# Background pieces spread by cost, GpSimd's sums on VectorE and ScalarE, and VectorE's products one matrix product later, in a four-layer encoder

## The chip, the cores and the metric

One core of a Trainium2 chip runs the whole program. Its engines are TensorE (PE in the views, PEld for its weight loads), VectorE (DVE), ScalarE (ACT) and GpSimd (POOL); SyncE (SP) issues the transfers between HBM and the on-chip memory. Each engine runs its own instructions in the order in which the program wrote them, and waits at an instruction until what that needs is there. The metric is the device time of one execution in microseconds (us), the median of several.

## The reference, cut to what matters

Four residual layers work on x of 512 positions by 1024 channels, in float32. Each is a token mixer (Fourier, S5 state space, dilated attention, Fourier) and then a dense SwiGLU layer of inner width 2816.

```python
def swiglu(h, w_gate_up, w_down):
    gate, up = jnp.split(h @ w_gate_up, 2, axis=-1)
    return (jax.nn.silu(gate) * up) @ w_down

for i in range(DEPTH):
    kind = i % N_MIXERS
    h = rms_norm(x, norm_mix_g[i])
    ... # Fourier, S5 or attention
    x = x + mix.astype(x.dtype)
    h = rms_norm(x, norm_ffn_g[i])
    x = x + swiglu(h, ffn_w_gate_up[i], ffn_w_down[i]).astype(x.dtype)
```

The S5 mixer also needs tables that hang on its parameters alone (powers of the complex eigenvalues times the input and output matrices, one set for each of 16 groups of four state blocks).

## The kernel before, in words

The activations stay in on-chip memory with channels on the partitions, X[:, m] being 128 channels by 512 positions, m = 0 to 7. The order on every engine is the order of the code. The plan is Fourier 0, feed-forward 0, S5, feed-forward 1, attention, feed-forward 2, Fourier 1, feed-forward 3.

**Products in two parts.** A float32 value is held as a high part of fewer bits and a low part, and a product is three matmuls (`mm3`, L338 to L340): high by high, high weight by low activation, low weight by high activation. `Stream` brings the weights in chunks of 128x1024: a transfer fills one of three raw buffers `wch`, ScalarE copies the high part into `whi` (L198), VectorE subtracts it to get `wlo` (L199), three buffers each. `next()` gives the chunk that is due and first splits up to two further ones. A transfer into a raw buffer waits until the split of the chunk three before it is done.

**Feed-forward layer (`ffn`).** Two halves. Each half has 11 pairs of products, gate f and up f, with one chunk and 24 matmuls each, into one of four accumulators `pg`. After both, VectorE scales each by the norm (L480, L483), ScalarE takes the SiLU; a product later VectorE multiplies them (L506), ScalarE copies the high part, and GpSimd subtracts to get the low part (L508) of `act`. Then come 8 down products of 33 matmuls, each added to X (L496) at its end; in the second half `after_x` prepares the next layer: squares on ScalarE (L399), their sum `acc` on GpSimd for m = 1 to 6 (L404, on VectorE for the last), and the scaled copy of X for the next layer (HH, high and low part: L434, L425; H for Fourier and S5). `norm_r` takes the sum of `acc` over the channels (L455) after the first two products of the next layer.

**Background.** The S5 tables are made inside feed-forward 0, the attention's bias tables inside feed-forward 1. They are a list of closures; `run_bg`, called after each of the 54 first slots (a slot is one product), runs about one of them. The S5 list is six pieces that ran in Fourier 0 (`run_front`), 14 pieces of set-up, and 40 half-steps: for group b, the loads come at step b, `inputs` (tables `wout`, `mph`) two steps on, `readers` (`bd`, `ce`) in the second half of that step, `lags` (48 small matmuls on TensorE, L974, and the stores) at step b+3, and the last stores at b+4.

**Fourier layer.** Two small transforms, and then for each m a pair of products `pq` and `pp`. ScalarE copies `pq` out (L691), GpSimd makes X - q and X + mirrored q (L693, L694), VectorE adds `pp` (L697, L698). GpSimd also folds the weights (`wplus`, L531).

## Time and profile before

| | |
|---|---|
| median of 3 runs | 2417.97 us (2413.87 to 2418.07) |
| the profiled execution | 2416.0 us |
| its span on the core | 2414.1 us |
| TensorE busy | 2327.1 us, 96% of the span |
| VectorE busy | 1361.5 us, 56% |
| ScalarE busy | 867.5 us, 36% |
| GpSimd busy | 274.9 us, 11% |

The busy shares are averages over stages with different limits, so they say little by themselves: each stage has to be read by its own stretch. The ends of matmuls are modelled, so a busy TensorE need not be one at its peak; what tells is the time that the same number of matmuls takes in two stretches, and the waits.

### The profile page before, as it was taken

What the parts mean: (1) busy time and instruction counts of PE and PEld (TensorE: products, weight loads), DVE (VectorE), ACT (ScalarE), POOL (GpSimd) and SP (SyncE); (2) the same over time, 40 slices, a digit from 0 to 9 for tenths busy, and PEclk for the clock granted to TensorE, in tenths of its full rate; (3) what the DMA queues carried; (4) which work ended last, traced back from release to release, by engine and by line L of the source; (5) the groups of instructions that cost most, each with busy time, mean ns of one, the idle gap of its engine ahead of it and who ended that gap; (6) DMA issues with size and microseconds to landing.
All of it is one profiled execution on the core that took longest, in us unless ns stands there. A gap on an engine that the chain in (4) does not pass through costs nothing.

```text
span 2414.1 us, 32242 instructions
## 1 busy us (share of the span) xinstructions
PE 2327.1 (96%) x12858; PEld 1925.5 (80%) x12858; DVE 1361.5 (56%) x2265; ACT 867.5 (36%) x1531; POOL 274.9 (11%) x213
## 2 busy tenths in 40 slices
PE   9999988968999999999999999999999999999999
PEld 7787766857878888889878987777888887888887
DVE  7878899487543333454576647774433337443332
ACT  3332222534233223244556446544322322322231
POOL 4210000152101001100000000002100115110110
PEclk9999999989999999999999999999999999999999
DMA  4257777783335444322232323232222232222222
GB/s 157 79 152 224 246 240 223 234 281 119 105 96 136 116 123 126 103 90 88 73 95 80 110 78 92 82 88 96 96 96 96 96 113 71 96 96 96 96 96 88
DMA packets 116490, 293.79 MB, mean 122 GB/s; under 512 B 23105, under 2 KB 50020, under 8 KB 116340
## 3 DMA queue, kind: packets, MB, share of 16 engines
q1 hardware_dynamic: 114804, 288.04, 38.3%
q10 hardware_dynamic: 1536, 3.70, 0.5%
q8 instruction: 101, 1.65, 0.3%
q14 instruction: 49, 0.40, 0.1%
HBM read 259.68 MB, written 36.21 MB: 123 GB/s over the span
## 4 chain that ended last, share of the span: by engine, by line
PE 81%; DVE 10%; DMA 3%; issue 2%; ACT 2%; SPq 1%; POOL 1%; ACTq 0%; DVEq 0%; POOLq 0%
PE pg L338 23%; PE pg L339 22%; PE pg L340 22%; PE pg L1392 2%; PE pg L1393 2%; PE pg L1394 2%; DVE wlo L199 1%; DMA s5ZS<-lt 1%; PE pt L1468 1%; PE pt L1510 1%; DVE ms L1113 1%; PE pt L628 1%; DVE ce L739 1%; PE pg L628 1%; PE pg L1435 1%
## 5 line engine op out<-in xcount | busy, mean ns | idle before, releaser
L199 DVE TENSOR_TENSOR wlo<-w,whi 128x1024 fp32r<-128x1024 f32 x360 | 450.8, 1255 | 574.7 <-ACT whi L198 574.7
L340 PE MATMUL pg<-HH,wlo 128*128 128x512 f32 x1792 | 703.2, 392 | 16.2 <-DVE wlo L199 16.2
L338 PE MATMUL pg<-HH,whi 128*128 128x512 f32 x1792 | 709.8, 396 | 3.4 <-DVE HH L434 3.4
L339 PE MATMUL pg<-HH,whi 128*128 128x512 f32 x1792 | 702.4, 392 | 2.0 <-DVE HH L425 2.0
L198 ACT CAST whi<-w 128x1024 fp32r<-128x1024 f32 x360 | 376.9, 1049 | 531.8 <-PE pg L339 420.1
L340 PEld LDWEIGHTS pg<-HH,wlo 128*128 128x128 f32 x1792 | 339.0, 189 | 91.3 <-DVE wlo L199 20.0
L338 PEld LDWEIGHTS pg<-HH,whi 128*128 128x128 f32 x1792 | 338.8, 189 | 81.2 <-DVE HH L434 5.2
L339 PEld LDWEIGHTS pg<-HH,whi 128*128 128x128 f32 x1792 | 339.0, 189 | 74.0 <-DVE HH L425 3.7
L340 PE MATMUL pg<-act,wlo 128*128 128x512 f32 x704 | 274.1, 389 | 1.0 <-DVE wlo L199 0.8
L339 PE MATMUL pg<-act,whi 128*128 128x512 f32 x704 | 274.1, 389 | 0.9 <-POOL act L508 0.9
L338 PE MATMUL pg<-act,whi 128*128 128x512 f32 x704 | 274.5, 390 | 0.0
L508 POOL TENSOR_TENSOR act<-t,act 128x512 fp32r<-128x512 f32 x88 | 115.8, 1316 | 1151.6 <-ACT act L507 1122.7
L483 DVE TENSOR_TENSOR t<-pg,r 128x512 f32<-128x512 f32 x88 | 60.6, 689 | 171.6 <-PE pg L340 171.6
L404 POOL TENSOR_TENSOR acc<-acc,sq 128x512 f32<-128x512 f32 x42 | 61.8, 1470 | 826.4 <-ACT sq L399 826.0
L340 PEld LDWEIGHTS pg<-act,wlo 128*128 128x128 f32 x704 | 132.1, 188 | 29.3 <-DVE wlo L199 1.8
L339 PEld LDWEIGHTS pg<-act,whi 128*128 128x128 f32 x704 | 132.1, 188 | 28.5 <-POOL act L508 1.2
L338 PEld LDWEIGHTS pg<-act,whi 128*128 128x128 f32 x704 | 132.1, 188 | 28.2 <-issue 0.9
L481 ACT ACTIVATE t<-t 128x512 f32<-128x512 f32 x88 | 55.7, 632 | 224.7 <-DVE t L480 224.7
L507 ACT CAST act<-t 128x512 fp32r<-128x512 f32 x88 | 54.7, 621 | 209.1 <-DVE t L506 209.1
L496 DVE TENSOR_TENSOR X<-X,pg 128x512 f32<-128x512 f32 x64 | 43.8, 685 | 89.3 <-PE pg L340 89.3
L1392 PE MATMUL pg<-whi,HH 128*128 128x256 f32 (+1 forms) x256 | 88.2, 344 | 0.0
L1393 PE MATMUL pg<-whi,HH 128*128 128x256 f32 (+1 forms) x256 | 87.1, 340 | 0.0
(331 smaller groups left out, 2723.5 us busy)
## 6 DMA issues: line engine op xcount, KB each, us to landing
w<-in_wgu_dram SPq DMA_DIRECT2D x176, 512.0 KB
w<-in_wdn_dram SPq DMA_DIRECT2D x88, 512.0 KB
w<-in_wqk_dram SPq DMA_DIRECT2D x48, 512.0 KB
w<-in_wv_dram SPq DMA_DIRECT2D x24, 512.0 KB
xpw<-s5SC SPq DMA_DIRECT2D x16, 512.0 KB
xbj<-in_bj_dram SPq DMA_DIRECT2D x16, 512.0 KB
s5WE<-wout SPq DMA_DIRECT2D x16, 512.0 KB
s5YW<-ce SPq DMA_DIRECT2D x16, 512.0 KB
```

The lines of the kernel that those rows point to most:

```text
L198: nc.scalar.copy(hi, t)
L199: nc.vector.tensor_tensor(lo, t, hi, ALU.subtract)
L338: mm(ps, wh, hh, start=first, stop=False)
L339: mm(ps, wh, hl, start=False, stop=False)
L340: mm(ps, wl, hh, start=False, stop=last)
L404: eng.tensor_tensor(self.acc, self.acc, sq, ALU.add)
L481: nc.scalar.activation(t1, t1, AF.Silu)
L483: nc.vector.tensor_tensor(t2, pp[1], self.r, ALU.mult)
L507: nc.scalar.copy(hi, t1)
L508: nc.gpsimd.tensor_tensor(lo, t1, hi, ALU.subtract)
L1392: mm(ps, x, wh[:, k], start=(kk == 0 and t % tb == 0), stop=False, skip_group_check=True)
L1393: mm(ps, y, wh[:, k], start=False, stop=False, skip_group_check=True)
```

## The change

What it does:

- Every background piece has a cost. `run_bg` gives 3 units of room to a gate or up slot, 5 to a down slot, and spreads the list over both halves up to the fourth down product of the second (`BG_ROOM`). An S5 half-step costs 5; the set-up pieces 31 together.
- The scaling of the up product, the multiplication and the low part come one product later than the scaling of the gate product. The low part is on VectorE.
- The low parts of weight chunks (`wlo`) are written after the products and the background piece of a slot (`hold`, `late_low`), no longer right behind the high part.
- A down product is added to X after the matmuls of the next one are written.
- GpSimd's other sums go to VectorE: `acc`, the fold `wplus`, the two sums of the Fourier layer, which now read `pq` directly. In the Fourier layer ScalarE makes the high part of HH, and four squares and sums come after the loop.
- The phases `mph` of the tables are made on ScalarE, four instructions for a group, one step earlier; the signs of `bd`, the copy of the lags and the last stores move to steps of their own.

```diff
+BG_ROOM = (3, 5, 4)
...
-        return len(r) < n or r[-n] < (self.nsplit if tag == "wch" and self.loaders[r[-n]][1] else free)
+        return len(r) < n or r[-n] < (self.nlow if tag == "wch" and self.loaders[r[-n]][1] else free)
...
-                nc.vector.tensor_tensor(lo, t, hi, ALU.subtract)
+                self.lows.append((lo, t, hi))
...
+            if not self.hold:
+                self.low()
+
+    def low(self):
+
+        while self.lows:
+            self.nc.vector.tensor_tensor(*self.lows.pop(0), ALU.subtract)
+        self.nlow = self.nsplit
+
+    def late_low(self):
+        self.low()
+        self._load(self.nuse - 1)
...
+    def run_bg(self, slots, down=False):
+
+        a, b, rest = BG_ROOM
+        self.due += self.total * (b if down else a) / ((4 * FH - 2) * a + (KT + rest) * b) if slots > 1 else self.total
+        while self.bg and self.due > 0:
+            cost, go = self.bg.pop(0)
+            self.due -= cost
+            go()
...
-            eng = nc.vector if m >= (7 if defer else KT - 1) else nc.gpsimd
-            eng.tensor_tensor(self.acc, self.acc, sq, ALU.add)
+            nc.vector.tensor_tensor(self.acc, self.acc, sq, ALU.add)
...
+            def product():
+
                 while late:
-                    self.split_mul(*late.pop())
+                    hi, lo, t1, ps = late.pop()
+                    t2 = wk.tile([P, S], F32, name="t2", tag="t2")
+                    nc.vector.tensor_tensor(t2, ps, self.r, ALU.mult)
+                    nc.vector.tensor_tensor(t1, t1, t2, ALU.mult)
+                    nc.scalar.copy(hi, t1)
+                    lows.append((lo, t1, hi))
+
+            def rest():
+
+                while lows:
+                    nc.vector.tensor_tensor(*lows.pop(), ALU.subtract)
...
             for hf in range(2):
+                self.stream.hold = True
                 for f in range(FH):
                     left = (2 - hf) * (2 * FH + KT) - 2 * f
-                    pp = [self.gemm(self.Hi, self.Lo)]
-                    finish()
+                    pg = self.gemm(self.Hi, self.Lo)
+                    product()
                     if f < FH - 1:
                         self.run_bg(left)
-                    pp.append(self.gemm(self.Hi, self.Lo))
+                    self.stream.late_low()
+                    pu = self.gemm(self.Hi, self.Lo)
...
-                    nc.vector.tensor_tensor(t1, pp[0], self.r, ALU.mult)
+                    nc.vector.tensor_tensor(t1, pg, self.r, ALU.mult)
                     nc.scalar.activation(t1, t1, AF.Silu)
...
+                    rest()
+                    late.append((act[:, 0, f, :], act[:, 1, f, :], t1, pu))
                     self.run_bg(left - 1)
+                    self.stream.late_low()
...
-                    if hf == 1 and m == 3 and nxt and nxt[1] == "s5":
+                    if m:
+                        result(m - 1, done, hf)
+                    self.run_bg((2 - hf) * (2 * FH + KT) - 2 * FH - m, True)
+                    if hf == 1 and m == 4 and nxt and nxt[1] == "s5":
                         self.s5_open()
...
-        nc.gpsimd.tensor_tensor(lo, t1, hi, ALU.subtract)
...
-                nc.gpsimd.tensor_tensor(wp[:, c], ta, tb, ALU.add)
+                nc.vector.tensor_tensor(wp[:, c], ta, tb, ALU.add)
...
-                nc.gpsimd.tensor_tensor(t1[:, 0:257], X[:, m, 0:257], q, ALU.subtract)
-                nc.gpsimd.tensor_tensor(t1[:, 257:512], X[:, m, 257:512], q[:, 255:0:-1], ALU.add)
...
+                nc.vector.tensor_tensor(t1[:, 0:257], X[:, m, 0:257], pq, ALU.subtract)
+                nc.vector.tensor_tensor(t1[:, 257:512], X[:, m, 257:512], pq[:, 255:0:-1], ALU.add)
...
+                squares.append(self.after_x(m, nxt, late=pool2, defer=True))
+                if m < 4:
+                    squares.pop(0)()
...
+                nc.scalar.activation(ph[:, g], sm["iota"], AF.Copy, scale=sm["phi0"][:, 4 * b + g:4 * b + g + 1])
...
-            tt(V, ph, phi.unsqueeze(2).to_broadcast([P, 4, 64]), sm["iota"].unsqueeze(1).to_broadcast([P, 4, 64]), M)
...
+        for i in range(22):
+            cost = 2 if i < 2 else 5 if i < 18 else 0.5
+            out.append((cost, step(i, ((4, lag_rows), (3, signs), (1, phases), (5, store), (2, inputs)))))
+            out.append((cost, step(i, ((3, lags), (4, lag_own), (5, spread), (2, readers), (0, loads)))))
```

How the order moves, first on VectorE in the second half of feed-forward 0, around one `inputs` half-step. In the kernel before, one slot from one weight split to the next:

```order
418 L199 TENSOR_TENSOR wlo<-w_2212,whi 128x1024
419 L506 TENSOR_TENSOR t_2371<-t_2371,t_2374 128x512
420 L739 TENSOR_TENSOR mph<-s5phi_316,c_iota 128x256
421 L931 TENSOR_SCALAR wtmp<-mph 128x4x64
422 L739 TENSOR_TENSOR mph<-mph,wtmp 128x256
423 L739 TENSOR_TENSOR wout<-xpw,xbj 128x4x128
424 L739 TENSOR_TENSOR wtmp<-xpw,xbj 128x512
425 L739 TENSOR_TENSOR wout<-wout,wtmp 128x4x128
426 L739 TENSOR_TENSOR wout<-xpw,xbj 128x4x128
427 L739 TENSOR_TENSOR wtmp<-xpw,xbj 128x512
428 L739 TENSOR_TENSOR wout<-wout,wtmp 128x4x128
429 L199 TENSOR_TENSOR wlo<-w_2297,whi 128x1024
```

In the changed kernel, a slot without a piece and then the slot of an `inputs` half-step:

```order
450 L214 TENSOR_TENSOR wlo<-w_2196,whi 128x1024
451 L520 TENSOR_TENSOR t_2494<-pg,r 128x512
452 L214 TENSOR_TENSOR wlo<-w_2253,whi 128x1024
453 L491 TENSOR_TENSOR t_2528<-pg,r 128x512
454 L492 TENSOR_TENSOR t_2494<-t_2494,t_2528 128x512
455 L967 TENSOR_SCALAR wtmp<-mph 128x4x64
456 L773 TENSOR_TENSOR mph<-mph,wtmp 128x256
457 L773 TENSOR_TENSOR wout<-xpw,xbj 128x4x128
458 L773 TENSOR_TENSOR wtmp<-xpw,xbj 128x512
459 L773 TENSOR_TENSOR wout<-wout,wtmp 128x4x128
460 L773 TENSOR_TENSOR wout<-xpw,xbj 128x4x128
461 L773 TENSOR_TENSOR wtmp<-xpw,xbj 128x512
```

The piece has lost its first instruction, and one slot in three now has no piece; before, every slot here had one. The scaling of the up product (L483, a row of the slot before this one in the old order) stands beside the multiplication.

On VectorE in the Fourier 0 layer, the sums of one m; in the kernel before:

```order
76 L199 TENSOR_TENSOR wlo<-w_391,whi 128x1024
77 L697 TENSOR_TENSOR X<-t_509,pt 128x257
78 L698 TENSOR_TENSOR X<-t_509,pt 128x255
79 L434 TENSOR_SCALAR HH<-X,c_gf 128x512
80 L425 SCALAR_TENSOR_TENSOR HH<-X,c_gf,HH 128x512
81 L789 TENSOR_SCALAR s5k<-s5a 128x128
```

and in the changed kernel:

```order
84 L214 TENSOR_TENSOR wlo<-w_391,whi 128x1024
85 L727 TENSOR_TENSOR t_503<-X,pg 128x257
86 L728 TENSOR_TENSOR t_503<-X,pg 128x255
87 L729 TENSOR_TENSOR X<-t_503,pt 128x257
88 L730 TENSOR_TENSOR X<-t_503,pt 128x255
89 L446 SCALAR_TENSOR_TENSOR HH<-X,c_gf,HH 128x512
90 L425 TENSOR_TENSOR acc<-acc,sq 128x512
91 L823 TENSOR_SCALAR s5k<-s5a 128x128
```

Two sums and an `acc` have come in, and the high part of HH (L434) has left.

On ScalarE in the last down products of feed-forward 0, where the phases `mt` of the S5 layer are turned into sines; in the kernel before (`whi` of chunks 72 and 73 are the layer's last two):

```order
206 L1023 ACTIVATE mt<-mt 128x512
207 L1024 ACTIVATE mt<-mt,c_cols 128x512
208 L198 CAST whi<-w_3933 128x1024
209 L198 CAST whi<-w_3970 128x1024
210 L399 ACTIVATE sq<-X 128x512
211 L1022 ACTIVATE mt<-mt 128x512
```

and in the changed kernel:

```order
210 L421 ACTIVATE sq<-X 128x512
211 L202 CAST whi<-w_3865 128x1024
212 L202 CAST whi<-w_3944 128x1024
213 L421 ACTIVATE sq<-X 128x512
214 L1072 ACTIVATE mt<-mt 128x512
215 L1073 ACTIVATE mt<-mt 128x512
```

Nine of the 24 `mt` instructions stood ahead of the two copies; now all stand behind them.

## Rows read from the trace of the kernel before

**Rows 1.** The page: the chain that ended last, shares of the span by engine.

```profile
PE 81%; DVE 10%; DMA 3%; issue 2%; ACT 2%; SPq 1%; POOL 1%; ACTq 0%; DVEq 0%; POOLq 0%
```

**Rows 2.** Windows: stretch, its length, busy (instructions), TensorE clock, DMA share, GB/s.

```profile
59.70:81.70 22.00, 16.59 (x52) 10.85 (x51) 20.53 (x39) 6.31 (x9) 8.93 (x8) 0.77 0.14 48
81.70:191.10 109.40, 109.40 (x486) 90.16 (x488) 85.59 (x167) 36.45 (x49) 12.82 (x11) 1.00 0.42 129
192.00:257.00 65.00, 64.17 (x416) 51.77 (x412) 58.18 (x102) 18.41 (x35) 2.58 (x2) 1.00 0.79 253
258.00:421.00 163.00, 142.67 (x1014) 110.98 (x1010) 151.65 (x263) 44.56 (x95) 12.99 (x9) 0.96 0.75 237
421.00:431.00 10.00, 8.94 (x81) 6.52 (x79) 6.62 (x8) 4.72 (x6) 2.58 (x2) 1.00 0.37 112
1754.90:1814.90 60.00, 60.00 (x266) 49.69 (x265) 19.66 (x21) 12.36 (x13) 1.29 (x1) 1.00 0.29 97
1814.70:1934.50 119.80, 119.80 (x530) 99.22 (x529) 47.19 (x54) 36.32 (x43) 12.89 (x10) 1.00 0.29 97
1994.50:2050.20 55.70, 53.61 (x265) 43.18 (x264) 41.03 (x69) 17.39 (x38) 33.99 (x26) 0.94 0.23 75
```

**Rows 3.** Waits of TensorE from 258 to 431 us: total, times, longest.

```profile
PE pg L340 <- DVE wlo L199: 16.2, 9, 2.4
```

**Rows 4.** Waits of TensorE from 59.7 to 82 us.

```profile
PE pg L338 <- DVE HH L434: 3.4, 2, 3.0
PE pg L339 <- DVE HH L425: 2.0, 2, 1.1
```

**Rows 5.** VectorE's instructions from 258 to 421 us: busy us, mean ns.

```profile
L199 DVE TENSOR_TENSOR wlo<-w,whi 128x1024 fp32r<-128x1024 f32 x22 | 26.8, 1218 | 0.0
L739 DVE TENSOR_TENSOR wout<-xpw,xbj 128x512 f32<-128x512 f32 x20 | 20.3, 1013 | 0.0
...
L739 DVE TENSOR_TENSOR wtmp<-xpw,xbj 128x512 f32<-128x512 f32 x20 | 13.6, 681 | 0.0
...
L480 DVE TENSOR_TENSOR t<-pg,r 128x512 f32<-128x512 f32 x10 | 6.8, 684 | 0.0
...
L739 DVE TENSOR_TENSOR mph<-s5phi,c_iota 128x256 f32<-128x256 f32 x10 | 4.2, 422 | 5.5 <-DMA s5PH<-mph 5.5
```

**Rows 6.** Timeline at 345 us, GpSimd and VectorE: start, length.

```profile
345.68 1.49 POOL L508 TENSOR_TENSOR act<-t,act 128x512 fp32r<-128x512 f32 x1 [14.16 <-ACT act L507]
...
345.94 1.78 DVE L739 TENSOR_TENSOR wout<-xpw,xbj 128x512 f32<-128x512 f32 x1
```

**Rows 7.** Timeline of TensorE around one block of `lags`.

```profile
280.93 0.39 PE L340 MATMUL pg<-HH,wlo 128*128 128x512 f32 x1
...
282.28 0.50 PE L338 MATMUL pg<-HH,whi 128*128 128x512 f32 x1
```

**Rows 8.** Timeline of VectorE around two set-up pieces (their first row, and what follows).

```profile
75.14 0.22 DVE L797 TENSOR_SCALAR s5mag<-s5rr 128x128 f32<-128x128 f32 x1
...
79.80 1.22 DVE L199 TENSOR_TENSOR wlo<-w,whi 128x1024 fp32r<-128x1024 f32 x1
```

**Rows 9.** Timeline where attention passes to feed-forward 2, GpSimd and TensorE.

```profile
1636.12 8.13 POOL L404 TENSOR_TENSOR acc<-acc,sq 128x512 f32<-128x512 f32 x6 [608.47 <-ACT sq L399]
...
1645.04 0.70 PE L455 MATMUL pt<-acc,c_ones 128*128 128x512 f32 x1 [2.59 <-DVE acc L404]
```

**Rows 10.** Timeline where Fourier 1 begins, VectorE and TensorE.

```profile
1997.29 4.79 DVE L410 TENSOR_SCALAR H<-X,c_gm 128x257 f32<-128x257 f32 x2
...
2002.14 0.80 PE L543 MATMUL pg<-c_cdft,H 128*128 128x128 f32 x2 [1.61 <-DVE H L410]
```

**Rows 11.** Timeline of ScalarE before S5.

```profile
468.48 1.98 ACT L198 CAST whi<-w 128x1024 fp32r<-128x1024 f32 x2
...
482.74 0.72 ACT L1024 ACTIVATE mt<-mt,c_cols 128x512 f32<-128x512 f32 x1
484.56 0.63 ACT L399 ACTIVATE sq<-X 128x512 f32<-128x512 f32 x1 [1.09 <-DVE X L496]
```

More of the change, by code (lines that the diff above doesn't have):

```diff
@@ L213, in next @@
         n = self.nuse
+        if n + count > self.nlow:
+            self.low()
         if ahead:
@@ L317, in set_bg @@
     def set_bg(self, closures):
-        self.bg, self.bg0, self.due, self.slots = list(closures), closures, 0, 4 * FH + KT + 2
-    def run_bg(self, slots):
-        self.due += len(self.bg0) / self.slots if slots > 1 else len(self.bg0)
-        while self.bg and len(self.bg0) - len(self.bg) < self.due:
-            self.bg.pop(0)()
+        self.bg, self.due, self.total = list(closures), 0, sum(c for c, _ in closures)
+    def run_bg(self, slots, down=False):
[5 more added lines that the diff above has]
+            go()
     def run_front(self):
         if self.front:
-            self.front.pop(0)()
+            self.front.pop(0)[1]()
     def keep_warm(self, count):
@@ L920, in c, with phases @@
             return d["bc"][:, 2 + i].unsqueeze(2).to_broadcast([P, 4, 8, 16])
+        def phases(b):
+            ph = tmp[b]["ph"] = tl("mph", [P, 4, 64], 3)
+            for g in range(4):
+                nc.scalar.activation(ph[:, g], sm["iota"], AF.Copy, scale=sm["phi0"][:, 4 * b + g:4 * b + g + 1])
         def inputs(b):
@@ L960, in readers, with signs @@
                 tt(V, ce[:, :, ri], ce[:, :, ri], t, Sb)
+        def signs(b):
+            bd = sm[f"bd{b % 2}"]
+            for di in range(2):
+                hs = slice(64 * di, 64 * di + 64)
+                for ri in range(2):
+                    nc.scalar.activation(bd[hs, 1 + di, ri, :, 0:16], bd[hs, 0, ri, :, 0:16], AF.Copy,
+                                         scale=1.0 - 2.0 * ri)
         def lags(b):
@@ L981, in lags, with lag_rows, lag_own, store @@
             nc.sync.dma_start(self.YW[k, h], ce.rearrange("p g r e q -> p (g r e q)"))
-        def last(b):
+        def lag_rows(b):
+            d = tmp[b]
+            lt = d["lt"] = tl("lt", [P, 256], 2)
+            cut = [t.rearrange("p (a x) -> p a x", a=2)[:, :, 0:112] for t in (lt, d["ps"])]
+            nc.scalar.copy(*cut)
+        def lag_own(b):
+            d = tmp[b]
+            tt(V, d["lt"][:, 112:128], d["ps"][:, 112:128], sm["dd"][:, b], A)
+        def store(b):
             k, h = divmod(b, 2)
@@ L1307, in attn_prepare @@
         out = [load, lambda: None, rows(0), rows(1), rows(2)]
-        return out + [copies(g, i) for g in range(3) for i in range(8)] + [st.close]
+        out += [copies(g, i) for g in range(3) for i in range(8)] + [st.close]
+        return [(1, f) for f in out]
     @staticmethod
```

71 lines of the change are left out of this document (26 added, 45 removed).

## The prediction

> **What bounds the kernel now.** I read the page first. TensorE holds 81% of the chain that ended last, so a gain can only come from stretches where it waits or runs at a lower clock [rows 1]. The windows then show where these are, since the four feed-forward layers do the same products. In feed-forward 2 the second half's 22 gate and up products take 119.8 us and its 8 down products 60.0, at full clock [rows 2]: 5.45 us a product, 7.5 a down product. The same 22 products of feed-forward 0 take 163.0 us. 11 blocks of `lags` lie between them; a block puts 1.35 us between two matmuls that else start 0.23 apart [rows 7], so 1.1 each, 12.1 in all. 163.0 - 119.8 - 12.1 = 31.1 us are lost. The waits say to whom: TensorE waits 16.2 us for the low parts of weights, nine times, all from VectorE [rows 3]. The mean clock of 0.96 (it has two levels, 2.4 and 1.2 GHz, and falls to the lower behind some of these waits) costs about 163.0 x 0.04 = 6.5 more. VectorE is busy 151.65 of the 163.0, so it is the bound there, and nowhere else for as long: in the first half's 109.4 us it was busy 85.59 and TensorE lost nothing [rows 2].
>
> Three smaller losses. The opening of feed-forward 0 takes 22.0 us for two products, 10.9 at full speed: 11.1 lost, 5.4 of it waiting for HH [rows 4], the rest clock (0.77). From 421 to 431 us, 10.0 for a down product (7.5) and a block (1.1): 1.4 lost. From 192 to 257 us, 65.0 for 60.0 and four blocks: 0.6. All told 44 us of feed-forward 0. Outside it, feed-forward 2 begins with a wait of 2.59 us for `acc` [rows 9], and Fourier 1 with one of 1.61 for H [rows 10].
>
> **The even spread (largest term).** The list is 31 units of set-up and 172 of half-steps, 203. The room is 42 x 3 + 12 x 5 = 186, so a gate or up slot gets 203 x 3 / 186 = 3.27 units and a down slot 5.5; before, each slot of the second half got a whole half-step (5 units). Three products then hold one group (10 units), where two held it.
>
> What a group costs VectorE: of the 151.65 us, splits take 26.8, the two scalings and the multiplication, alike in shape, 6.8 each [rows 5]; 104.5 is left for 10.5 groups, 10.0 each. Two parts of that vanish. The first `mph` goes to ScalarE (4.2 / 10 = 0.42; ScalarE is busy 44.56 of 163.0, so four instructions a group hide there). And GpSimd stops holding VectorE up: a `wout` that starts inside GpSimd's 1.49 us instruction takes 1.78 us [rows 6]. The mean is 1013 ns for `wout` and 681 for `wtmp`, which has the same shape [rows 5], so 0.33 x 20 = 6.6 us here, 0.63 a group. That leaves 8.95. Three products then ask of VectorE 8.95 + 3 splits of 1.22 + six sums of 0.684 (per pair two scalings, one multiplication and the low part that comes from GpSimd) = 16.7 us, and of TensorE 3 x 5.45 + 1.1 = 17.4. So VectorE drops just below TensorE, with 4% to spare.
>
> The pieces stay lumps: a slot with one holds 4.5 + 1.4 + 1.2 = 7.1 us, two in a row 14.2 against 12.0 of TensorE, and then one of 2.6. This is covered, since the split made in a product's slot is wanted two products (10.9 us) later. If that cover were gone, each group would cost 2 us. VectorE's waits for TensorE shrink as well: the up product's scaling, which stood ahead of the piece, now comes a product later, when its matmuls are done. I leave 2 us lost of the 31.1 (bounds 0 and 22, the latter under the first rival): **-29**. The 1.4 and 0.6 go too: the low part of `act` is then made in 0.68 instead of 1.49 and is wanted only at the end of the first down product. **-2.0**.
>
> The transfers gain the same evenness. The down products of the first half take five groups instead of four; they ran at 253 GB/s and a share of 0.79, so this rises to about 0.9. It stays below one, and weights are asked for two products ahead.
>
> **The opening of feed-forward 0.** VectorE comes out of the Fourier tail earlier, as it is no longer held up, and the wait for the last HH should shrink to about 1 us. But the set-up now comes three times as dense: 4 units took 75.14 to 79.80, 4.66 us [rows 8], so 3.27 units are 3.8, and with 1.4 of sums and a split of 1.2 a slot asks 6.4 us against 5.45. Over 31 / 3.27 = 9.5 slots this is 9 us behind. The cover is thin at the layer's start, and one or two falls of the clock add to it; the wait for HH and the cover that there is take off as much. So I put the loss at 9 instead of 11.1 (bounds 1, if most is covered, and 14): **-2.1**.
>
> **GpSimd's other sums.** Ahead of feed-forward 2 six sums take 8.13 us on GpSimd [rows 9]; on VectorE, at 0.68 each, they keep up with the squares (0.63, [rows 11]), so `acc` is there before TensorE asks: **-2.6** (1.5 to 3.2). At the start of Fourier 1 two H instructions take 4.79 us [rows 10] while GpSimd folds weights; with the folds behind them the wait of 1.61 goes, and of the clock's loss (55.7 x 0.06 = 3.3 over the stretch) about a quarter: **-2.5** (1.6 to 3.5). In the tail VectorE takes on 16 half-wide sums (6.4 at 0.4), seven of `acc` (4.8) and four folds (4.9), less eight high parts: 41.03 + 16 - 5 = 52 of 55.7 us, and less again as it is not held up. So it stays off the path, where TensorE is. One fold now stands ahead of VectorE's first work on the path in Fourier 0: **+0.5** (0 to 1.2).
>
> **The order on ScalarE before S5.** The nine `mt` instructions that stood ahead of the last two weight copies (468.48) now follow them. The second copy cannot begin before the matmuls of its buffer's last chunk end, three chunks (16.4 us) before the layer's end, so the copies end about where they began before, at 468.5. The 24 `mt` and two squares behind them last some 17.2 us, to 485.7, where the last square began at 484.56 [rows 11]. S5 needs that square: **+1.2** (0 to 3).
>
> **The sum.** -29.1 - 2.0 - 2.1 - 2.6 - 2.5 + 0.5 + 1.2 = -36.6 from the execution's 2416.0 (span 2414.1 and 1.9 around it) is 2379.4. The median of the three runs is 2.0 above that execution, so I say 2380.
>
> **Rivals.** First: VectorE stays the bound through the whole layer. It now idles 7% of the 163.0 us though it is the bound; if it goes on doing so, 16.7 becomes 18.0, and if GpSimd's hold were not the cause of the long `wout`, 18.7. That is 1.3 us over TensorE's 17.4 for each of 17 groups, 22 us lost instead of 2: 2400. The thin 4% speaks for it; that the idling came with waits which the new order takes away speaks against. The Trainium skill (Perfetto Trace Analysis, Optimizing Scalar/DVE Operations) says that a saturated VectorE may be relieved by moving work to ScalarE or GpSimd, though it doubts the latter because the two share a port; the change moves work the other way, and by the first half of that rule it would end near this rival, by the rows on `wout` near the forecast. Chance 18%.
>
> Second: the spread does not do what it is for. If TensorE waits for each lump, not for the average, the 16 groups cost 1.8 us each (16.2 / 9) wherever they stand; 29 us come back, and the time is 2408 to 2416. Against it: in the first half, where some half-steps already ran in slots of the old order, TensorE lost nothing in 109.4 us. 6%.
>
> Third, slower than before: VectorE pays GpSimd's price for what it takes over. The place is the two Fourier layers: 41.03 + 33.99 = 75.0 us in 55.7, 19.3 over in each; in feed-forward 0 the low part at 1.4 instead of 0.68 us, 1.5 times a group, turns 16.7 into 17.8, 0.4 over TensorE's 17.4 in each of 17 groups, 7 us. 38.6 + 7 = 46 on top of 2380 is 2426. It decides where 38 of the 46 are paid, what the forecast gains. Against it is that the same shape takes 0.68 on VectorE [rows 5]. 4%.
>
> **How the numbers follow.** The likeliest case, 70%, has its own range of 2367 (nothing lost among the groups, 1 us at the opening, the best of the other bounds) to 2392 (14 at the opening and half the first rival's loss). With the first rival the range of 2366 to 2402 holds about 8 in 10. 0.2%, about 5 us, is what a measurement of this kernel can tell from no change. Faster: 70 + 18 + 2 (part of the second) + 2 for mixtures = 92%. Same 4%, slower 4%.
>
> **What would show it.** In the second half of feed-forward 0, 22 products and some seven blocks in about 130 us with no row of long waits for `wlo`, VectorE busy above 90%; `wout` at 0.69 us in the mean. Small waits for `wlo` in the first 60 us of the layer. No wait ahead of feed-forward 2, H in Fourier 1 at under 0.5 us an instruction. The last square before S5 about 2 us behind the last matmul. It would be wrong if waits for `wlo` or for weights run through the whole layer, or if the Fourier layers take more than 56 us.

## The result, and the profile after

The changed kernel takes 2386.26 us (median of four runs, 2384.55 to 2388.79) beside 2417.46 for the kernel before on the same chip (2413.87 to 2418.07): a ratio of 0.9875, 95% interval 0.9858 to 0.9892. The forecast was 2380, range 2366 to 2402. The profiled execution of the changed kernel, the slowest of the four, took 2388.79 us, span 2386.4.

The page of the changed kernel: the chain that ended last, by engine.

```profile
PE 85%; DVE 9%; ACT 3%; issue 2%; DMA 1%; POOL 0%; ACTq 0%; SPq 0%; DVEq 0%; POOLq 0%
```

TensorE holds 85% of it, where it held 81 [rows 1]. The windows of the changed kernel, cut where feed-forward 0 passes from its first two products to the rest of the gate and up products, the down products, the second half's gate and up products and its down products; then Fourier 1 and attention (columns as in [rows 2]).

```profile
64.80:79.40 14.60, 12.50 (x52) 8.98 (x51) 13.82 (x35) 7.65 (x10) 0.37 (x2) 1.00 0.12 36
79.40:199.30 119.90, 114.67 (x578) 92.53 (x577) 104.94 (x212) 43.66 (x73) 0.00 (x0) 0.99 0.55 170
199.30:264.20 64.90, 64.90 (x458) 52.70 (x457) 57.12 (x102) 22.24 (x57) 0.00 (x0) 1.00 0.75 234
264.20:392.70 128.50, 128.50 (x866) 104.65 (x865) 116.06 (x200) 50.00 (x106) 0.00 (x0) 1.00 0.74 243
392.70:461.30 68.60, 65.31 (x409) 52.86 (x407) 39.39 (x64) 27.53 (x46) 0.00 (x0) 0.98 0.75 242
1971.40:2022.00 50.60, 50.38 (x266) 40.16 (x264) 38.16 (x84) 17.34 (x34) 0.00 (x0) 1.00 0.25 83
1009.40:1611.20 601.80, 588.03 (x3858) 501.77 (x3857) 381.14 (x892) 308.91 (x747) 0.80 (x4) 0.99 0.28 88
```

The second half's gate and up products now take 128.5 us: 22 products of 5.45 and 7 blocks of 1.1 are 127.6, so under 1 us is lost, and VectorE is busy 116.06, not the bound. What is still lost lies at both ends of the layer: 3.7 us in the first two products (14.6 for 10.9, where 11.1 were lost before), 8.7 in the next 20 (119.9 for 109.0 and two blocks) and 5.3 in the last down products (68.6 for 60.0 and three blocks). TensorE's waits in feed-forward 0 say to whom.

```profile
PE pg L362 <- DVE wlo L214: 5.2, 3, 2.1
PE pt L1012 <- ACT s5bd L998: 3.3, 1, 3.3
PE pg L361 <- DVE HH L446: 2.1, 2, 1.0
```

The 16.2 us for `wlo` in the second half [rows 3] are gone, the three waits that are left lie at 81, 89 and 124 us. The wait for `s5bd` is new. Two of the waits draw a fall of the clock behind them, as does the end of the layer: windows of the changed kernel.

```profile
124.80:128.30 3.50, 3.45 (x8) 2.75 (x9) 1.90 (x4) 2.04 (x4) 0.00 (x0) 0.53 0.75 194
428.50:432.00 3.50, 3.47 (x52) 2.85 (x53) 0.52 (x2) 0.45 (x2) 0.00 (x0) 0.54 1.02 367
465.90:472.70 6.80, 6.80 (x50) 5.30 (x52) 1.89 (x3) 2.83 (x5) 0.00 (x0) 0.53 0.95 277
```

At a mean granted clock of 0.53 to 0.54 (nearly all of the stretch at the lower level, 1.2 GHz) 3.5 us lose about 1.6, 6.8 lose 3.2. Some of VectorE's instructions from 264.2 to 392.7 us, by form, beside [rows 5]:

```profile
L214 DVE TENSOR_TENSOR wlo<-w,whi 128x1024 fp32r<-128x1024 f32 x21 | 25.6, 1218 | 0.0
L773 DVE TENSOR_TENSOR wout<-wout,wtmp 128x512 f32<-128x512 f32 x16 | 11.1, 692 | 0.6
L773 DVE TENSOR_TENSOR wout<-xpw,xbj 128x512 f32<-128x512 f32 x15 | 10.3, 684 | 0.0
L773 DVE TENSOR_TENSOR wtmp<-xpw,xbj 128x512 f32<-128x512 f32 x15 | 10.3, 684 | 0.0
```

`wout` has come down from 1013 ns to 684. By stage, the two profiled executions compare as follows (each stage from its first matmul to that of the next):

| stage | before, us | after, us | difference | forecast |
|---|---|---|---|---|
| Fourier 0 | 59.7 | 64.8 | +5.1 | +0.5 |
| feed-forward 0 | 424.1 | 396.6 | -27.5 | -33.1 |
| S5 and its gate | 180.3 | 185.4 | +5.1 | +1.2 |
| feed-forward 1 | 362.7 | 362.7 | 0.0 | 0 |
| attention | 604.7 | 601.9 | -2.8 | 0 |
| feed-forward 2 | 363.0 | 360.1 | -2.9 | -2.6 |
| Fourier 1 | 55.8 | 50.6 | -5.2 | -2.5 |
| feed-forward 3 | 363.9 | 364.3 | +0.4 | 0 |

Three places need their rows. Near the end of feed-forward 0, VectorE, ScalarE and TensorE of the changed kernel around the new wait:

```profile
426.28 0.68 DVE L502 TENSOR_TENSOR X<-X,pg 128x512 f32<-128x512 f32 x1
...
427.05 0.63 ACT L421 ACTIVATE sq<-X 128x512 f32<-128x512 f32 x1 [3.62 <-DVE X L502]
427.59 0.33 ACT L1022 COPY lt<-pt 128x224 f32<-128x224 f32 x1
427.81 0.81 ACT L998 ACTIVATE s5bd<-s5bd 64x64 f32<-64x64 f32 x4
...
428.53 0.80 PE L1012 MATMUL pt<-ce,s5bd 128*32 128x112 f32 x16 [3.29 <-ACT s5bd L998]
```

The signs of `bd` for the last group stand on ScalarE behind the square of X. The square waits 3.62 us for VectorE's sum into X, and on VectorE that sum stands behind a whole `readers` piece and a split. The last step of the list costs only 0.5 units, so signs and lags fall into one slot and TensorE is at the lags at once. ScalarE at the end of the layer, and TensorE behind it:

```profile
444.82 1.05 ACT L202 CAST whi<-w 128x1024 fp32r<-128x1024 f32 x1 [4.38 <-PE pg L361]
448.12 0.63 ACT L421 ACTIVATE sq<-X 128x512 f32<-128x512 f32 x1 [2.24 <-DVE X L502]
448.66 0.61 ACT L1072 ACTIVATE mt<-mt 128x512 f32<-128x512 f32 x1
...
465.22 0.61 ACT L421 ACTIVATE sq<-X 128x512 f32<-128x512 f32 x1
...
465.89 3.32 PE L1101 MATMUL pt<-sq,c_zone 128*128 128x64 f32 x16 [1.47 <-ACT sq L421]
```

The last copy ends at 445.87, 15.4 us before the last matmul (461.3). ScalarE then waits another 2.24 us for X, so the 24 `mt` and the squares run to 465.8, 4.5 us behind the last matmul; before it was 1.4 (485.19 and 483.7, [rows 11]). In Fourier 0, the fold that now stands ahead of VectorE's first work waited 2.87 us for its weights. TensorE then waited 1.58 us, for what the profile doesn't tell, and a fall of the clock followed:

```profile
17.77 1.23 DVE L566 TENSOR_TENSOR wplus<-w,w 128x1024 f32<-128x1024 f32 x1 [2.87 <-DMA w<-in_fwb_dram]
...
20.15 0.68 PE L642 MATMUL pt<-c_csn,T 128*128 128x129 f32 x4 [1.58 <-issue]
```

### The profile page after: what moved, and what is told of

It reads as the page before. It is cut to its first block, busy times and chain, and to the rows that moved or that the text cites. A ratio compares the mean times of both kernels' runs of the same rounds, so it can differ in the third digit from the quotient of the medians.

```text
span 2386.4 us, 32286 instructions
## 1 busy us (share of the span) xinstructions
PE 2316.7 (97%) x12858; PEld 1921.6 (81%) x12858; DVE 1395.4 (58%) x2403; ACT 884.5 (37%) x1595; POOL 48.4 (2%) x43
## 4 chain that ended last, share of the span: by engine, by line
PE 85%; DVE 9%; ACT 3%; issue 2%; DMA 1%; POOL 0%; ACTq 0%; SPq 0%; DVEq 0%; POOLq 0%
PE pg L360 24%; PE pg L361 23%; PE pg L362 23%; PE pg L1443 2%; PE pg L1444 2%; PE pg L1445 2%; PE pt L1519 1%; DVE wlo L214 1%; PE pt L663 1%; PE pt L1561 1%; DVE ms L1163 1%; PE pt L1012 1%; PE pg L663 1%; PE pt L1581 1%; DMA wb<-wrow 1%
## 5 line engine op out<-in xcount | busy, mean ns | idle before, releaser
L214 DVE TENSOR_TENSOR wlo<-w,whi 128x1024 fp32r<-128x1024 f32 x360 | 438.7, 1220 | 342.5 <-ACT whi L202 342.3
L491 DVE TENSOR_TENSOR t<-pg,r 128x512 f32<-128x512 f32 x88 | 60.7, 690 | 194.1 <-PE pg L362 194.1
L520 DVE TENSOR_TENSOR t<-pg,r 128x512 f32<-128x512 f32 x88 | 60.6, 689 | 186.4 <-PE pg L362 170.0
L1445 PE MATMUL pg<-wlo,HH 128*128 128x256 f32 (+1 forms) x256 | 87.1, 340 | 0.0
L1473 ACT ACTIVATE qsq<-tqk 128x512 f32<-128x512 f32 x48 | 30.3, 631 | 143.5 <-DVE tqk L1466 101.6
L521 ACT ACTIVATE t<-t 128x512 f32<-128x512 f32 x88 | 55.8, 634 | 41.8 <-DVE t L520 41.6
```

The costliest lines, as they stand in the source:

```text
L214: self.nc.vector.tensor_tensor(*self.lows.pop(0), ALU.subtract)
L491: nc.vector.tensor_tensor(t2, ps, self.r, ALU.mult)
L520: nc.vector.tensor_tensor(t1, pg, self.r, ALU.mult)
L521: nc.scalar.activation(t1, t1, AF.Silu)
L1445: mm(ps, x, wl[:, k], start=False, stop=(kk == KT - 1), skip_group_check=True)
```

## The experiments

All times are medians of four runs beside the kernel before on the same chip: 2414.93 us for before_even, one_piece, gpsimd_sums and gpsimd_folds, 2414.27 for last_lag, phases_early, setup_price and mended, 2414.65 for scale_at_once, low_at_once, gpsimd_acc and priced. Since that differs from the 2417.46 beside the changed kernel, kernels are compared with it by their ratios. The interval of a ratio reaches some 0.0015, 3.6 us, to either side; kernels closer than that are told apart only by the windows of their profiles, one execution each. The table gives what is lost in feed-forward 0, by the stretches of the windows above: the length less 5.45 us a product (7.5 a down product) and 1.1 a block of lags, each figure good to some 0.2 us.

| kernel | us | ratio to before, 95% interval | first two | next 20 | down 0 | second half | down 1 | layer |
|---|---|---|---|---|---|---|---|---|
| before | 2417.46 | 1 | 11.1 | 0.1 | 1.6 | 31.8 | 1.9 | 424.1 |
| changed | 2386.26 | 0.9875 (0.9858 to 0.9892) | 3.7 | 8.7 | 0.5 | 0.8 | 5.3 | 396.6 |
| before_even | 2400.53 | 0.9942 (0.9927 to 0.9957) | 11.0 | 3.7 | 2.8 | 3.3 | 10.0 | 408.4 |
| one_piece | 2394.68 | 0.9917 (0.9900 to 0.9933) | 5.2 | 0.8 | 0.5 | 21.5 | 0.0 | 405.5 |
| gpsimd_sums | 2386.32 | 0.9882 (0.9868 to 0.9897) | 5.2 | 10.4 | 0.5 | 0.8 | 6.6 | 401.0 |
| gpsimd_folds | 2387.32 | 0.9888 (0.9873 to 0.9903) | 3.6 | 8.7 | 0.5 | 0.8 | 5.4 | 396.5 |
| scale_at_once | 2393.32 | 0.9911 (0.9895 to 0.9928) | 5.3 | 15.5 | 0.5 | 2.7 | 7.1 | 408.6 |
| low_at_once | 2385.13 | 0.9880 (0.9865 to 0.9895) | 5.0 | 5.7 | 2.2 | 0.8 | 5.4 | 396.7 |
| gpsimd_acc | 2388.59 | 0.9892 (0.9877 to 0.9906) | 3.8 | 8.7 | 0.5 | 0.8 | 5.4 | 396.7 |
| last_lag | 2380.82 | 0.9860 (0.9843 to 0.9878) | 3.8 | 12.0 | 0.5 | 0.9 | 0.3 | 395.0 |
| phases_early | 2383.96 | 0.9872 (0.9857 to 0.9888) | 5.2 | 10.2 | 0.9 | 0.8 | 6.9 | 401.5 |
| setup_price | 2378.01 | 0.9844 (0.9828 to 0.9859) | 3.8 | 1.9 | 0.4 | 0.9 | 5.5 | 390.0 |
| mended | 2380.16 | 0.9852 (0.9830 to 0.9873) | 3.8 | 5.7 | 1.7 | 2.2 | 0.3 | 391.3 |
| priced | 2374.76 | 0.9834 (0.9820 to 0.9849) | 3.8 | 1.8 | 0.5 | 1.3 | 0.4 | 385.4 |

### before_even: the spread alone, on the kernel before

```diff
-        self.due += len(self.bg0) / self.slots if slots > 1 else len(self.bg0)
-        while self.bg and len(self.bg0) - len(self.bg) < self.due:
-            self.bg.pop(0)()
+        self.due += self.total * (b if down else a) / ((4 * FH - 2) * a + (KT + rest) * b) if slots > 1 else self.total
+        while self.bg and self.due > -1e-6:
+            cost, go = self.bg.pop(0)
```

> The kernel before with one thing alone of the change: its pieces carry costs and are spread by them over both halves (one group of tables in three products, not in two); GpSimd's sums and the order on VectorE stay. If evenness is what pays, three products ask 10.0 + 3 x 1.22 + 4.5 x 0.684 = 16.7 us of VectorE and 17.4 of TensorE, so nearly all of the 28 us lost in the second half of feed-forward 0 come back, and the opening loses 1 to 3 more, the set-up being denser: 2390 to 2397. Rival: without GpSimd's work gone, or with the scaling of the up product still ahead of the piece, the waits for wlo go on: 2403 to 2417.

The second half's windows and waits in this kernel:

```profile
265.20:396.20 131.00, 129.31 (x866) 104.29 (x864) 116.20 (x191) 39.98 (x75) 12.19 (x9) 1.00 0.73 231
...
PE pg L345 <- DVE wlo L200: 1.7, 3, 0.7
```

The waits for `wlo` fall from 16.2 us to 1.7 with GpSimd and the order on VectorE as they were: of the 31 us, the spread alone gives back 28.5. The whole kernel gains only 14.4 (2414.93 to 2400.53), because 12.8 more are lost elsewhere in the layer (3.6 at the denser set-up, 1.2 and 8.1 in the down products; in the last ones TensorE waits 4.1 us, in two waits, for `ce`). The theory is confirmed for the second half; the total is 3.5 us above its band.

### one_piece: the change without the spread

```diff
-BG_ROOM = (3, 5, 4)
+BG_ROOM = (1, 1, 4)
...
-        return out + [(0, end2)]
+        return [(1, f) for _, f in out] + [(1, end2)]
```

> The changed kernel with every piece at the same cost and every slot with the same room (some 1.1 pieces a slot, as before), all else kept. If evenness is what pays, two products ask 8.95 + 2 x 1.22 + 4 x 0.684 = 14.1 us of VectorE and 12.0 of TensorE: 2 us lost in each of 8 to 10 groups of the second half, and 1 to 3 us won back at the opening: 2400 to 2408. Rival: the moves off GpSimd and the new order pay: 2384 to 2390, with no waits for wlo in the second half.

```profile
253.40:405.90 152.50, 137.78 (x1013) 107.83 (x1010) 135.24 (x240) 52.19 (x125) 0.00 (x0) 0.98 0.78 249
...
PE pg L362 <- DVE wlo L214: 14.1, 7, 4.0
```

Window and waits of the second half: the waits are back, and 21.5 us are lost there in ten groups, about the 2 us a group that were worked out. The rest of the change is thus worth about 10 of the 31 us when the lumps stay. But the total is only some 10 over the changed kernel (0.9917 beside 0.9875), not the 14 to 22 expected, and lies between the theory's band and the rival's: without the spread the opening loses 0.8 in its 20 products instead of 8.7, and the last down products nothing instead of 5.3. The spread wins 20.7 us in the middle and pays 11.7 of it back at the ends of the layer.

### gpsimd_sums: low parts of `act` and `acc` on GpSimd again

```diff
-                    nc.vector.tensor_tensor(*lows.pop(), ALU.subtract)
+                    nc.gpsimd.tensor_tensor(*lows.pop(), ALU.subtract)
...
-            nc.vector.tensor_tensor(self.acc, self.acc, sq, ALU.add)
+            eng = nc.vector if late or m == KT - 1 else nc.gpsimd
+            eng.tensor_tensor(self.acc, self.acc, sq, ALU.add)
```

> The changed kernel with the low part of act, and the sums acc outside the Fourier layers, on GpSimd again. VectorE idled about 19 of 172 us in the second half of feed-forward 0, and each of 16 low parts may hold it 1.1 us but takes 0.68 off it, so if there is cover that stretch loses 0 to 5 us, and feed-forward 2 begins 2.6 us later: 2388 to 2394. Rival: GpSimd's hold was the cause of the waits before: 15 us or more come back there, 2401 or over. Third: the acc on VectorE is worth nothing: 2386.

The sums ahead of feed-forward 2 were left on VectorE by this edit (they go by the argument `late`), so it says nothing of that stage; gpsimd_acc does. The total, below the theory's band and at the third's 2386, hence does not show what the sums ahead of feed-forward 2 are worth. In the second half the same 0.8 us is lost. VectorE's instructions there, in this kernel:

```profile
L774 DVE TENSOR_TENSOR wtmp<-xpw,xbj 128x512 f32<-128x512 f32 x15 | 13.6, 904 | 0.0
L774 DVE TENSOR_TENSOR ct<-s5ei,bc 128x512 f32<-128x512 f32 x14 | 12.9, 919 | 0.0
L774 DVE TENSOR_TENSOR wout<-wout,wtmp 128x512 f32<-128x512 f32 x16 | 11.1, 692 | 0.6
```

GpSimd now holds up `wtmp` and `ct` instead of `wout`: 0.22 x 15 + 0.235 x 14 = 6.6 us, and the ten low parts that VectorE was spared are 6.8. The two cancel: moving them is worth nothing for VectorE's busy time (117.28 us in this stretch, 116.06 in the changed kernel's). At the ends of the layer it may be worth something: the layer takes 401.0 us in this profile, with 3 us more lost at the opening and 1.3 at the end, while it takes 396.5 to 396.7 in the three profiles of the changed kernel, gpsimd_folds and gpsimd_acc. The ratio (0.9882 beside 0.9875) is too coarse to confirm or rule out 4 us.

### gpsimd_folds: the weight folds on GpSimd again

```diff
-                nc.vector.tensor_tensor(wp[:, c], ta, tb, ALU.add)
+                nc.gpsimd.tensor_tensor(wp[:, c], ta, tb, ALU.add)
```

> The changed kernel with the folds wplus on GpSimd again. If the first fold, which waits 2.9 us for its weights at the head of VectorE, is what makes Fourier 0 five us longer (64.8 for 59.7), that layer falls back to 59.5 to 61.5; if the folds on GpSimd were what slowed H at the start of Fourier 1, that layer rises from 50.8 to 53 to 56. Together 2384 to 2389. Rival: the sums of the Fourier loop on VectorE made both differences; then both layers stay within 0.7 us of 64.8 and 50.8.

Fourier 1 takes 54.3 us instead of 50.6. Its start in this kernel, VectorE, GpSimd and TensorE:

```profile
1967.76 4.79 DVE L431 TENSOR_SCALAR H<-X,c_gm 128x257 f32<-128x257 f32 x2
...
1964.92 7.47 POOL L566 TENSOR_TENSOR wplus<-w,w 128x1024 f32<-128x1024 f32 x3 [959.52 <-PE pg L362]
...
1972.61 0.51 PE L578 MATMUL pg<-c_cdft,H 128*128 128x128 f32 x2 [1.61 <-DVE H L431]
```

The same two H instructions take 4.79 us as in [rows 10], with the same wait of 1.61; in the changed kernel they take 0.61 and nothing waits. A fall of the clock comes with it (0.97 in the mean over the layer, 1.00 in the changed kernel). So 3.7 of the 5.2 us are the folds; what made the other 1.5 was not tried.

Fourier 0 takes 60.7. But that is no proof that the fold made the 64.8: in the eight other kernels that keep the first fold on VectorE (all but gpsimd_folds, mended, priced and before_even) the layer took 60.2 to 61.4, and with it on GpSimd 59.7 to 61.1 (the kernel before and before_even among them). In one_piece it waited 1.27 us for its weights, not 2.87:

```profile
16.28 1.22 DVE L566 TENSOR_TENSOR wplus<-w,w 128x1024 f32<-128x1024 f32 x1 [1.27 <-DMA w<-in_fwb_dram]
```

In all eight the fold waited 1.05 to 1.32 us and began by 17.2 us, and TensorE had no wait there; in the profiled execution it began at 17.77. That the late weights made TensorE's wait and the 64.8 is thus likely, and not shown.

### scale_at_once, low_at_once: the order on VectorE, in its two parts

```diff
-                    late.append((act[:, 0, f, :], act[:, 1, f, :], t1, pu))
+                    t2 = wk.tile([P, S], F32, name="t2", tag="t2")
+                    nc.vector.tensor_tensor(t2, pu, self.r, ALU.mult)
+                    late.append((act[:, 0, f, :], act[:, 1, f, :], t1, t2))
```

> The changed kernel with the up product scaled at once, ahead of the next piece, as before the change; only the multiplication stays a product later. In the kernel before with the even spread alone this order left 1.7 us of waits for wlo in the second half, so its own worth in feed-forward 0 is small: 396.6 to 399 us. Rival: VectorE waits for the up product's end with the piece and wlo queued behind it, and three products no longer hold a group: 404 us or more, with waits for wlo in the second half.

Neither came about as put. The layer takes 408.6 us, 12 more, as the rival has it, but only 1.9 of them are lost in the second half; the opening loses 20.8 instead of 12.4. TensorE's waits from 60.6 to 204 us:

```profile
PE pg L362 <- DVE wlo L214: 9.4, 5, 3.8
PE pg L361 <- DVE HH L446: 2.0, 2, 1.0
```

VectorE's scaling of the up product up to the first down product, first in this kernel, then in the changed one:

```profile
L522 DVE TENSOR_TENSOR t<-pg,r 128x512 f32<-128x512 f32 x10 | 6.9, 687 | 14.0 <-PE pg L362 14.0
```

```profile
L491 DVE TENSOR_TENSOR t<-pg,r 128x512 f32<-128x512 f32 x10 | 6.8, 684 | 0.8 <-PE pg L362 0.8
```

With the scaling ahead of the piece, VectorE can begin a dense set-up piece only when the up product has ended, and `wlo` stands behind both: VectorE waits 14.0 us for up products there where it waited 0.8. Where a slot is not overfull (the second half) the wait is made up; where it is, it comes through. The late scaling is worth 12 us here, most of it by softening the set-up.

```diff
-                self.stream.hold = True
+                self.stream.hold = False
```

> The changed kernel with wlo written right behind its whi again, ahead of the products and the piece of a slot. VectorE then waits at wlo for ScalarE's copy, but wlo comes sooner behind a long piece, so the waits at the opening (5.2 us in three) may even shrink: feed-forward 0 393 to 398 us. Rival: the place of wlo behind the piece is what keeps the second half free: waits of 5 us or more appear there, 402 or more.

The layer takes 396.7 us and the second half loses the same 0.8: the late `wlo` alone is worth nothing, as its theory said. The waits for `wlo` in the first half's gate and up products fall to 2.4 us, but the down products lose 2.2 instead of 0.5.

### last_lag, phases_early, setup_price: one loss each

```diff
-            cost = 2 if i < 2 else 5 if i < 18 else 0.5
+            cost = 2 if i < 2 else 5 if i < 19 else 0.5
```

> The changed kernel with the piece of the last group's signs and lags at 5 units instead of 0.5 (steps below 19, not 18), so that the two no longer fall into one slot. If TensorE's wait of 3.3 us for the signs of bd near the end of feed-forward 0 comes from that slot, where ScalarE first waits for a square and that for VectorE, it goes with the fall of the clock behind it (1.7): feed-forward 0 391 to 393 us instead of 396.6. Rival: ScalarE's squares hold the signs up in any down slot; then a wait of 2 us or more stays there.

```profile
393.90:456.40 62.50, 62.49 (x361) 50.91 (x359) 30.70 (x46) 26.82 (x42) 0.00 (x0) 1.00 0.72 231
```

Window of the last down products: 62.5 us, no wait and no fall of the clock; the 5.3 us are gone, so they were that slot's. The opening, with the list slightly denser, lost 3.3 us more (12.0), which is why the layer stands at 395.0, above the band. The ratio falls by 0.0015, 3.6 us, about what it can tell.

```diff
-                for k in range(3 * m - 12, min(3 * m - 9, KT) if m < 7 else 0):
+                for k in range(3 * m - 9, min(3 * m - 6, KT) if m < 6 else 0):
...
-                    if hf == 1 and m == 4 and nxt and nxt[1] == "s5":
+                    if hf == 1 and m == 3 and nxt and nxt[1] == "s5":
```

> The changed kernel with S5 opened one down product earlier and the phases mt turned into sines behind results 3 to 5 instead of 4 to 6 (the pieces end one down product earlier too, room 3, 5, 3). If the 24 mt that stand behind the last two weight copies are what delays the last square (4.5 us behind the last matmul, 1.45 before the change) and lowers the clock behind it, the stretch from there to the end of S5's gate falls from 185.4 to 180.3 to 182, feed-forward 0 stays within 1.5 of 396.6. Rival: the transfers of the phases collide with the weights, or the square waits for X alone: less than 1.5 won.

S5 and its gate fall from 185.4 to 180.9 us, what they took before the change. ScalarE there:

```profile
459.67 0.62 ACT L421 ACTIVATE sq<-X 128x512 f32<-128x512 f32 x1
463.28 0.63 ACT L421 ACTIVATE sq<-X 128x512 f32<-128x512 f32 x1 [3.00 <-DVE X L503]
```

The `mt` are done before the layer's end, and the last square, at 463.28 for matmuls that end at 462.5, waits for X alone. In this kernel the theory holds for S5. For feed-forward 0, which was to stay within 1.5 us, it doesn't: the layer takes 401.5, as the pieces must end a slot earlier, the list is denser, and the opening loses 3 us more, the last down products 1.6. Over the whole kernel hardly anything is won (0.9872), the rival's size: S5 gains 4.5 us and feed-forward 0 loses 4.9.

```diff
+        out = [(1.4 * c, f) for c, f in out]
         for i in range(22):
```

> The changed kernel with the set-up pieces priced 1.4 times as high, so that they come less dense and the half-steps closer (3.47 units a slot instead of 3.27, a group in 2.88 products: 8.95 + 2.88 x 2.59 = 16.4 us of VectorE against 16.8 of TensorE). If the waits for wlo at the opening (5.2 us, and 1.7 of clock) come from set-up pieces too dense for a slot, most go: feed-forward 0 390 to 393. Rival: the second half has no room for it: waits for wlo of 5 us or more appear there, and the layer stays at 395 or over.

```profile
75.50:187.60 112.10, 110.82 (x531) 91.04 (x530) 98.71 (x200) 43.79 (x73) 0.00 (x0) 1.00 0.51 156
253.50:382.10 128.60, 128.60 (x870) 104.71 (x865) 120.23 (x208) 50.95 (x114) 0.00 (x0) 1.00 0.81 255
```

Windows of the 20 products at the opening and of the second half: the 20 products lose 1.9 instead of 8.7 (TensorE's waits for `wlo` in the layer fall from 5.2 us to 1.3), the second half still 0.9, with VectorE at 120.23 of 128.6. The theory is confirmed; by the ratio (0.9844) 7.5 us are won.

### gpsimd_acc: the sums ahead of feed-forward 2

```diff
-            nc.vector.tensor_tensor(self.acc, self.acc, sq, ALU.add)
+            eng = nc.gpsimd if tuple(nxt) == (2, "ffn") and m < KT - 1 else nc.vector
+            eng.tensor_tensor(self.acc, self.acc, sq, ALU.add)
```

> The changed kernel with the sums acc ahead of feed-forward 2 alone (m = 1 to 6) on GpSimd again. If their 1.36 us against 0.78 on VectorE made the wait of 2.59 us there, feed-forward 2 goes from 360.1 back to 362.5 to 363.2, the rest stays. Rival: the squares, two of which can be open, set the pace, or something else of the change made that stage shorter: 360 to 361.

```profile
PE pt L477 <- DVE acc L426: 2.6, 1, 2.6
```

The wait of [rows 9] is back, and feed-forward 2 takes 363.0 us, what it took before the change. Of the other stages only Fourier 0 (61.4) and attention (603.4) differ by more than 1 us from the changed kernel's, and these two vary between profiles of the same order. The theory is confirmed.

### mended, priced: together

mended holds last_lag, phases_early, setup_price and the first fold on GpSimd; priced leaves the phases where the change has them and prices only the last signs, not the lags.

```diff
-            out.append((cost, step(i, ((4, lag_rows), (3, signs), (1, phases), (5, store), (2, inputs)))))
+            out.append((5 if i == 18 else cost, step(i, ((4, lag_rows), (3, signs), (1, phases), (5, store), (2, inputs)))))
```

> The changed kernel with these three together, and the first fold of Fourier 0 on GpSimd as before. If the terms add: 5 (signs), 4.5 (phases), 5 (set-up), 0 to 4 (the fold, where its weights come late): 2368 to 2375. Rival: with fewer slots for all pieces the second half turns over to VectorE and gives half of it back: 2376 to 2382.

> The changed kernel with the set-up priced 1.4 times as high, the last group's signs at 5 units in a slot ahead of its lags, and the first fold of Fourier 0 on GpSimd; S5 is opened where the change opens it. If the terms of the single runs add (8 by the set-up's price, 4 to 5 by the signs), 2371 to 2375. Rival: at 3.55 units a slot (a group in 2.82 products: 16.25 us of VectorE, 16.5 of TensorE) lumps of the second half come through as waits: 2376 to 2382.

The windows of the second half, first of mended, then of priced:

```profile
259.10:389.00 129.90, 128.95 (x871) 104.61 (x865) 125.16 (x218) 49.44 (x110) 0.00 (x0) 1.00 0.82 254
```

```profile
253.10:382.10 129.00, 128.96 (x869) 104.62 (x866) 121.48 (x209) 51.18 (x115) 0.00 (x0) 1.00 0.82 258
```

The terms don't add in mended (2380.16, its rival): with the pieces ending a slot earlier VectorE is busy 96% of the second half, and waits of 4.1 us for `wlo` come through in the layer. Nor do the early phases keep what they won: S5 and its gate take 184.4 us here, where they took 180.9 in phases_early. ScalarE's last two squares in mended, whose last matmul of the layer ends at 451.5:

```profile
451.62 0.61 ACT L421 ACTIVATE sq<-X 128x512 f32<-128x512 f32 x1
454.15 0.63 ACT L421 ACTIVATE sq<-X 128x512 f32<-128x512 f32 x1 [1.92 <-DVE X L503]
```

The last square ends 3.3 us behind that matmul, in phases_early 1.4. There the last down products took 69.1 us, here 62.5, so ScalarE has less time for the `mt` ahead of the layer's end; part of the 4.5 us won in phases_early seems to hang on the time lost just before, which no run tries by itself. priced keeps VectorE at 94% and loses 7.8 us in the whole layer. At 2374.76 (0.9834) it beats both kernels, the changed one by some 10 us, within its theory's band. Not tried were priced with the early phases but without the earlier end, and, each by itself, three parts of the change: the sum into X a product later, the phases on ScalarE, and the sums of the Fourier layers on VectorE.

## Why the prediction was right

The direction, the range and the largest term were right, and none of the three rivals came. The first wanted 18.0 to 18.7 us of VectorE for three products; VectorE idles 10% of the second half and 0.8 us is lost. The second wanted TensorE to wait for each lump wherever it stands; before_even has the lumps, GpSimd and the old order, and waits 1.7 us. The third wanted 1.4 us for what VectorE takes over; the low part of `act` runs at 681 ns in the second half, and Fourier 1 has become shorter. One sign of being wrong, Fourier layers of more than 56 us, was badly put: it can only mean Fourier 1 (50.6), since Fourier 0 took 59.7 before the change.

**The even spread**, -29: measured -31.0 (31.8 lost, now 0.8). Shown from both sides: the spread alone takes the loss to 3.3, all else without the spread only to 21.5. My working put the loss at 31.1 because it counted 11 blocks of lags between these products; by the trace ten start there. What my sum of VectorE's time booked as a gain, the end of GpSimd's hold of 0.63 a group, is used up by the low parts that VectorE took on for it, 1.5 x 0.684 a group: gpsimd_sums shows the two cancelling.

**The down products**, -2.0: measured +2.3. The first half's went as forecast (1.6 to 0.5; I had 0.6 for the 1.6, counting as its fourth block one that starts at 256.98 and ends outside the window), but the second half's lose 5.3 where 1.9 were lost. The failed step is "The 1.4 and 0.6 go too": it looked at the low part of `act` alone. The signs of `bd`, which the change moves to a step of their own on ScalarE, got no wait in my working, though the order shows the square ahead of them and the list the price of 0.5 that puts signs and lags into one slot. last_lag takes the whole 5 us away. The first half's down products also took four blocks, not five groups, at a transfer share of 0.75, not 0.9; nothing hung on that.

**The opening**, -2.1, bounds -10 to +3: measured +1.2 (11.2 to 12.4), within the bounds. The place and the cause were right (setup_price takes 6.8 of it away); the term was mis-sized, 9 for what is 12.4. A unit of set-up costs VectorE more than one of a half-step: by the trace `factors1`, 2 units, runs from 84.95 to 88.00 us, 1.5 us a unit, `powers`, 3 units, from 112.42 to 115.79, 1.1, and a `readers`, 5 units, from 420.49 to 425.23, 0.95.

**S5's opening**, +1.2, bounds 0 to 3: measured +5.1. The copies end where I put them, 15.4 us before the last matmul (I had 468.5 beside 483.7, 15.2), and the `mt` behind them make the last square late. The step that failed is that the `mt` begin at once: ScalarE first waits 2.24 us for X, and the square ends 4.5 us behind the last matmul where I had 2.0. My 1.2 also set the end of that square (485.7) against the start of the one before (484.56, its end 485.19). And I left out the clock, which falls behind the late square and costs some 3.2 by its row. The nine other kernels with this order take 183.7 to 186.4 us, so it is no chance of one execution. phases_early takes 4.5 away, but mended, with the same early phases, only 1.0: how much is the place of the `mt` alone stays open.

**The sums from GpSimd**: ahead of feed-forward 2, -2.6, measured -2.9, shown by gpsimd_acc. Fourier 1, -2.5, measured -5.2: all of the clock's loss came back and not a quarter of it; 3.7 are shown to be the folds. Fourier 0, +0.5, bounds 0 to 1.2: +5.1 in the profiled execution, but 60.2 to 61.4 us in the eight other kernels with that fold, against 59.7 to 61.1 with it on GpSimd; the 5.1 belongs to one execution, whose weights came late, and the fold's own price is too small to see.

**Attention**, to which my sum gave nothing, is 2.8 us shorter. It isn't the change: behind the same wait of 3.08 us for `ptr` the clock falls in the kernel before (at 1261 us) and in nine of the twelve experiments, and doesn't in the changed kernel's profile; the stage takes 600.2 to 604.9 us over the profiles of the changed kernel and the experiments, 604.7 before.

Without attention's and Fourier 0's chance, the errors are +4.3 in the down products, +3.3 at the opening, +3.9 at S5, -2.0 in the second half, -2.7 in Fourier 1: 6.8 in all, of which the median shows 6.3. The prediction is right for the most part by its own steps. That its errors came in both signs is luck, though the three upward ones alone, 11.5, would have left the time in the range.

## What to carry to other kernels

Spread background work by its cost on the engine that takes it, not by its count: here that alone gave back 28.5 of 31.8 lost us, and the moves off GpSimd added nothing that could be seen on that stretch. But price every kind of piece from the trace; what is priced too low (set-up at 1.1 to 1.5 us a unit beside 0.95, a last step at 0.5) moves the stall to both ends of the layer, and two such prices set right (with the first fold back on GpSimd) were worth another 10 us. And when an instruction is moved to another engine's queue, look at what stands ahead of it there: here a square that waits for a sum that waits for a whole piece.

## What the runs showed of the hardware that I had not expected

VectorE's 128x512 sums and products with both operands in on-chip memory (SBUF) take longer when GpSimd's 1.5 us instruction runs beside them, and which of them it is depends on what stands there: `wout` before (1013 ns in the mean), `wtmp` and `ct` in gpsimd_sums (904 and 919), each 683 or 684 without. What VectorE saves by giving a sum to GpSimd (0.68 us) it lost again in waiting (0.66). The scalings `t<-pg,r`, which have one operand in the matmuls' own memory (PSUM), stay at 686 to 687 ns there. The two H instructions of Fourier 1, with one operand from SBUF and a column, are slowed too: 4.79 us beside GpSimd's fold, 0.61 without. The Trainium skill (SBUF — State Buffer, Who interferes with whom) has it so for the instructions with two operands: a VectorE instruction with two SBUF inputs contends with a GpSimd instruction that reads SBUF, and whichever comes first blocks the other; this trace agrees ([rows 6]: a `wout` that starts 0.26 us into GpSimd's 1.49 us takes 1.78). That the trade is even, and not a gain, is this case's number, for this stretch.

The same wait of TensorE, 3.08 or 3.09 us at the same instruction of attention, is followed by a lower clock in ten of the fourteen profiles and not in the other four. Attention takes 600.2 us in last_lag's profile and 604.9 in one_piece's, its instructions being the same, at a mean granted clock of 0.99 and 0.98.
